# S5 state space layer: the products "powers times B" one f tile ahead, and the states turned into matmul operands by a ScalarE copy and a trip through DRAM

## The chip, the core and the metric

The kernel runs on one NeuronCore of a Trainium2 chip. The metric is the device time of one execution in microseconds (us). In the names used here TensorE is PE (the matrix engine; PEld is its weight load), VectorE is DVE, ScalarE is ACT, GpSimd is POOL and SyncE is SP. A matmul's result lands in PSUM, everything else that an engine reads or writes lies in SBUF, both with 128 partitions; weights and intermediate arrays lie in DRAM and move by DMA. Each engine works through its own list of instructions in order and waits for the others by semaphores. PE, DVE and ACT compute; SP only issues DMAs, and ACT and POOL can issue them too.

## The reference

Two layers, each a token mixer in a wide projection with a gate, then a residual and a LayerNorm: first chunked gated linear attention (GLA), then a complex diagonal state space layer (S5). The change lies in the second. Cut to what matters:

```python
# u_in: (1, 256, 2048); 256 groups of 16 channels, 64 complex states each
u, z = jnp.split(u_in @ w_in, 2, axis=-1)              # 2048 -> 4096 and 4096
dt = jnp.exp(log_dt)[:, None]
lam = exp(a_re * dt) * (cos(a_im * dt) + i sin(a_im * dt))   # written out in real parts
bb = (lam - 1) / (a_re + i a_im) * b                   # per group 64 x 16, complex
bu = einsum('blgi,gpi->blgp', u, bb)
x_l = lam * x_{l-1} + bu_l                             # associative_scan over 256 frames
y = einsum('blgp,gip->blgi', x_r, c_re) - einsum('blgp,gip->blgi', x_i, c_im) + d_skip * u
y = jax.nn.gelu(y)
y = y * jax.nn.sigmoid(y @ w_glu + b_glu)
return (y * jax.nn.silu(z)) @ w_out
```

The first half of `w_in`'s columns gives the input u, the second half the gate z.

## The kernel before, in words

**Weights.** All large weight matrices are float32 and are streamed once, in tiles of 128 partitions x 1024 (512 KB each, loaded by SP, L134). `split` makes two parts of each tile: `hi`, a copy rounded to the format fp32r (an ACT cast, L145), and `lo`, the rest (a DVE subtraction, L146). The activations are kept in the same two parts. A product is then three fast matmuls, hi x hi, lo x hi and hi x lo (`st_step`, L180 to L182, 24 matmuls for one weight tile). There are four buffers for the loaded tiles and three each for `hi` and `lo`. For every step of a projection ACT must cast, DVE must subtract, and only then PE can end the step.

**The S5 layer's recurrence** is cut into 32 chunks of 8 frames. The 4096 channels make 32 f tiles of 128 channels (8 groups of 16), and 16 pairs p of such tiles. Within a chunk everything is a matrix product, and only the state at the chunk's end goes from chunk to chunk. This needs, for each f tile:
- "powers times B" (`b_pow`): B times eight powers of lambda. One ACT copy and three DVE products (L1096 to L1098, by `powmul`'s and `b_pow`'s lines) make the buffer `wb` from the record `rb`.
- `b_tr`: eight PE transposes of it (L1107) into PSUM `pswb`, and two ACT copies.
- `s_mm` for a pair: matmuls for the chunks' own state and for the kernel of the first eight frames, PSUM `pss`; a DVE transpose (L1139) puts the states into `sx`, the large state array.
- `k_out`: the kernel of eight frames goes out to DRAM (`dk`).
- `scan`: 30 steps for each half h of the f tiles, three small DVE instructions each (L1187 to L1189), in place in `sx`.
- `cside`: the records of C and lambda are loaded (`cl`, three DMAs), the block Toeplitz operand `mt` is read back from `dk` (L1233, 512 KB, two buffers), and `powmul` makes C times powers (`wc0`, `wc1`).
- `xstage` (L1238 to L1247): the states of the chunks' starts are made an operand: a DVE transpose from `sx` to `xT` (L1241), two PE transposes to PSUM `psxs` (L1244), an ACT copy to `xS` (L1246).
- `ystage` (L1249 to L1263): 24 matmuls in PSUM `psy` (8 with `mt`, L1256, 16 with `wc` and `xS`, L1259), a DVE transpose to `yt` (L1262), and gelu on ACT back into `U` (L1263).

**What runs when.** This work runs in the gaps of two projections of 8 groups g by 8 steps kp. The input projection `su` (L1198 on) takes a queue `bq` of the B work: `bstep` runs as many entries at each step as `b_pace` allows, which is set to -4 at the start of g = 1 (so the queue starts some steps later, when u's first tiles are there) and gains 1 a step. From g = 4 on, `pump` also runs scan steps of half 0. The gate projection `sz` (L1274 on) ends the queue in g = 0 and then pumps a second queue `bg`, filled in the order of f: up to three scan steps of half 1, `cside(f)`, `xstage(f - 1)`, `ystage(f - 2)`; `Y_RATE` = 2.311 entries a step. The gate's silu (L1284, `zs`) stands at the end of each g.

The order in which this text runs gives a priority; a scheduler then sets each engine's list from the priorities, its own costs of instructions and the buffers' turnover, so the lists may differ from the text. Buffers are tiles of pools: a tile with `bufs=n` takes the n places in turn and waits until the place is free. `s8` is a pool of 12 large places that `wu`, `wb`, `U`, `zs` and others share.

Of the kernel before, what the change touches and what calls it, by code (L numbers as in the profile page):

```python
# [15 lines left out]
P = 128  # L16
# [17 lines left out]
def trunk(ctx, tc, x, c, ln_g, ln_b, ada_w, ada_b, gla_w_in, gla_gate_w2, gla_gate_b, gla_norm_g,  # L34
# [394 lines left out]
    vt = cp.tile([P, 104], F32, name="vt")  # L429
    gnT, gbT, bgluT, lngT, lnbT = vt[:, 0:32], vt[:, 32:40], vt[:, 40:72], vt[:, 72:88], vt[:, 88:104]  # L430

    def vectors():
# [8 lines left out]
        S.copy(vt, ps[:, :104])  # L441

# [5 lines left out]
    abT = cp.tile([P, 64], F32, name="abT")  # L448
# [22 lines left out]
    dT = cp.tile([16, 256], F32, name="dT")  # L471

    def prep_small():
# [5 lines left out]
        S.copy(dT, ps[:16, 0:256])  # L479
# [121 lines left out]
    def prep_pow(t):  # L601
# [14 lines left out]
        wdma(rec[:, 16 * t:16 * t + 16, 128:256], lc.rearrange("p f r g n -> p f (r g n)"))  # L616

    def to_rows(src, i_of, t, o, nm):
        got = {}

        def step(ib):
# [7 lines left out]
            if ib == 3:  # L629
                av = a.rearrange("p (f g) i -> p f (g i)", f=16)  # L630
                wdma(rec[:, 16 * t:16 * t + 16, o:o + 128], av)

        return [lambda ib=ib: step(ib) for ib in range(4)]

    def prep_b(t):
# [22 lines left out]
        return [load], [comp] + to_rows(lambda: got["b"], lambda s, i: s[:, :, i], t, 256, f"b{t}")  # L658

    def prep_c(t):  # L660
# [15 lines left out]
        return [load], [comp] + to_rows(lambda: got["c"], lambda s, i: s[:, i].rearrange("g r p -> g (r p)"), t, 0, f"c{t}")  # L676
# [15 lines left out]
    Y_RATE = 2.311  # L692
# [360 lines left out]
    def bload(f2):  # L1053

        a = tp.tile([P, 2, 384], F32, tag="rb", name=f"rb{f2}", bufs=2)
        dma(a[:, :, 0:256], rec[:, 2 * f2:2 * f2 + 2, 128:384])
        for h in range(2):
            dma(a[64 * h:64 * h + 64, :, 256:384], rec[64 - 64 * h:128 - 64 * h, 2 * f2:2 * f2 + 2, 256:384])
        rb[f2] = a
# [3 lines left out]
    def kload(f2):  # L1063

        a = rc[f2] = tp.tile([P, 2, 144], F32, tag="rc", name=f"rc{f2}", bufs=2)
        dma(a, rec[:, 2 * f2:2 * f2 + 2, 0:144])

    wb = {}
# [10 lines left out]
    wu, kts, Upair = {}, {}, {}  # L1079

    def b_pow(f):
        p = f // 2
        if f % 2 == 0:
# [3 lines left out]

            wu[p] = s8t(f"wb{p}", [2, 8, 16, 8])
        a = rb[p][:, f % 2]
        w = wu[p][:, f % 2]  # L1090
# [9 lines left out]
    def b_tr(f):  # L1100
        p = f // 2
        if f % 2 == 0:
            wb[p] = s8t(f"wbt{p}", [2, 8, 128])
        for h in range(2):
            ps = psx(f"pswb{f}{h}")
            for g in range(4):
                PE.transpose(ps[:, g * P:(g + 1) * P], wu[p][:, f % 2, 4 * h + g].rearrange("p i s -> p (i s)"), ident)  # L1107
            S.copy(wb[p][:, f % 2, 4 * h:4 * h + 4, :], ps.rearrange("p (g r) -> p g r", g=4))
# [10 lines left out]
    def s_mm(p):  # L1119
        pss = [psx(f"pss{2 * p + i}") for i in range(2)]  # L1120
        for i in range(2):
# [4 lines left out]
            for b in range(2):  # L1126
                for q in range(4):
                    PE.matmul(pss[i][32 * q:32 * q + 32, b * P:(b + 1) * P], lhsT=U[:, 2 * q + b],
                              rhs=wb[p][:, i, 2 * q + b, :], start=True, stop=True)
# [326 lines left out]
```

## Time and profile before

| | |
|---|---|
| time, median of 3 runs | 1836.67 us (1836.52 to 1839.31) |
| profiled execution | 1838.83 us, span 1837.1 us |
| granted TensorE clock, mean | 0.991 |
| ACT, POOL busy | 895.4 us (49%), 88.0 us (5%) |
| DMA | 457.86 MB, 249 GB/s over the span; 437.01 MB read, 18.61 MB written |
| of the chain that ended last | PE 78%, DVE 11%, DMA 4%, issue 3%, ACT 2% |

Busy time is the sum of an engine's instructions; an engine that is not busy either waits for a semaphore or for its own issue. A window is a stretch of the span in microseconds from its start; its row gives the length, then each engine's busy time with the count of its instructions, the granted clock, the mean busy share of the 16 DMA engines and the rate. A row of waits reads: waiting engine, tile and line, releaser with its tile and line, then microseconds in total, times, longest. A row of groups reads: line, engine, operation, output and input with their sizes, count, busy time in us, mean ns of one, and idle time before it with what ended it. Timeline rows begin with start and duration. The stages that the change touches lie, by the first and last matmul of each, at 762 to 1019 us (`su`) and 1021 to 1289 us (`sz`).

### The profile page before, as it was taken

To read this page: it belongs to the slowest core of one execution; us is meant where nothing else is said; L and a number is where in the kernel's file an instruction comes from. 1 tells how busy PE (TensorE), PEld (TensorE's weight loads), DVE (VectorE), ACT (ScalarE), POOL (GpSimd) and SP (SyncE) were. 2 spreads that over 40 slices of the span, in tenths; PEclk is the share of its full clock that TensorE was granted. 3 is DMA by queue.
4 is the path that set the end of the run, shared out by engine and by line. 5 is a ranking of instruction groups with operands and counts; after the bars stand their busy time and mean duration, and the time that the engine had idled before them with its cause. 6 is when DMAs were issued, how large, how long until landed. Compare 5 with 4: busy or idle time off the path is not lost.

```text
span 1837.1 us, 33664 instructions
## 1 busy us (share of the span) xinstructions
PE 1781.8 (97%) x13491; PEld 1574.5 (86%) x13491; DVE 1410.3 (77%) x1880; ACT 895.4 (49%) x1266; POOL 88.0 (5%) x94
## 2 busy tenths in 40 slices
PE   7999999999999999999999999999999999999997
PEld 5776897899999888899998999988888888888886
DVE  4887757879999988687699689888577775557556
ACT  4433557556556333654554535545445444444332
POOL 0000000000000000002233300000000000000000
PEclk9999999999999999999999999999999999999998
DMA  9997975879889998486665577999688886668653
GB/s 343 387 342 247 294 247 162 284 258 325 290 289 321 335 356 289 160 264 204 194 202 168 170 213 217 234 246 233 218 278 269 275 271 208 187 192 324 194 185 92
DMA packets 246101, 457.86 MB, mean 249 GB/s; under 512 B 19828, under 2 KB 49198, under 8 KB 244662
## 3 DMA queue, kind: packets, MB, share of 16 engines
q1 hardware_dynamic: 239320, 436.02, 74.1%
q0 software_dynamic: 5856, 18.63, 3.1%
q8 instruction: 106, 1.74, 0.4%
q10 hardware_dynamic: 768, 1.05, 0.2%
q14 instruction: 51, 0.42, 0.1%
HBM read 437.01 MB, written 18.61 MB: 248 GB/s over the span
## 4 chain that ended last, share of the span: by engine, by line
PE 78%; DVE 11%; DMA 4%; issue 3%; ACT 2%; POOL 0%; SPq 0%; DVEq 0%; ACTq 0%; POOLq 0%
PE gl L192 13%; PE gl L193 7%; PE op L168 6%; PE op L169 6%; PE op L167 6%; PE z L182 3%; PE z L181 3%; PE z L180 3%; PE v L168 3%; PE v L169 2%; PE v L167 2%; PE su L180 2%; PE su L181 2%; PE su L182 2%; PE sz L180 2%
## 5 line engine op out<-in xcount | busy, mean ns | idle before, releaser
L146 DVE TENSOR_TENSOR logl<-wgl,higl 128x1024 fp32r<-128x1024 f32 x128 | 156.7, 1224 | 116.0 <-ACT higl L145 111.2
L145 ACT CAST higl<-wgl 128x1024 fp32r<-128x1024 f32 x128 | 134.4, 1051 | 172.4 <-PE gl L192 167.5
L192 PE MATMUL gl<-yp,higl 128*128 128x512 f32 x512 | 179.4, 395 | 0.1
L192 PE MATMUL gl<-yb,higl 128*128 128x512 f32 x512 | 179.1, 395 | 0.0
L145 ACT CAST hio<-wo 128x1024 fp32r<-128x1024 f32 x95 | 100.2, 1055 | 152.8 <-PE op L169 131.9
L146 DVE TENSOR_TENSOR loo<-wo,hio 128x1024 fp32r<-128x1024 f32 x95 | 116.5, 1228 | 66.8 <-ACT hio L145 64.8
L317 DVE SCALAR_TENSOR_TENSOR acc<-wa,cs,acc 128x512 f32<-128x512 f32 x217 | 162.7, 750 | 2.9 <-DMA wa<-in_ada_w 0.2
L180 PE MATMUL sz<-u1h,hisz 128*128 128x256 f32 x512 | 150.4, 294 | 2.3 <-ACT zs L1284 2.3
L180 PE MATMUL su<-u1h,hisu 128*128 128x256 f32 x512 | 151.3, 297 | 0.0
L180 PE MATMUL z<-u0h,hiz 128*128 128x256 f32 x512 | 148.7, 290 | 0.0
L182 PE MATMUL sz<-u1h,losz 128*128 128x256 f32 x512 | 144.5, 283 | 2.1 <-DVE losz L146 2.1
L182 PE MATMUL su<-u1h,losu 128*128 128x256 f32 x512 | 145.8, 285 | 0.0
L181 PE MATMUL su<-u1l,hisu 128*128 128x256 f32 x512 | 145.6, 284 | 0.0
L182 PE MATMUL z<-u0h,loz 128*128 128x256 f32 x512 | 144.9, 283 | 0.6 <-DVE loz L146 0.6
L181 PE MATMUL z<-u0l,hiz 128*128 128x256 f32 x512 | 144.7, 283 | 0.0
L181 PE MATMUL sz<-u1l,hisz 128*128 128x256 f32 x512 | 144.7, 283 | 0.0
L193 PE MATMUL gl<-yb,logl 128*128 128x256 f32 x512 | 143.0, 279 | 0.0
L193 PE MATMUL gl<-yp,logl 128*128 128x256 f32 x512 | 142.3, 279 | 0.0
L145 ACT CAST hisz<-wsz 128x1024 fp32r<-128x1024 f32 x64 | 67.0, 1049 | 113.6 <-PE sz L181 57.4
L192 PEld LDWEIGHTS gl<-yp,higl 128*128 128x128 f32 x512 | 95.9, 188 | 22.9 <-issue 0.6
L192 PEld LDWEIGHTS gl<-yb,higl 128*128 128x128 f32 x512 | 96.0, 188 | 22.6
L145 ACT CAST hiz<-wz 128x1024 fp32r<-128x1024 f32 x64 | 67.2, 1051 | 88.2 <-PE z L181 80.8
(322 smaller groups left out, 5000.8 us busy)
## 6 DMA issues: line engine op xcount, KB each, us to landing
wgl<-in_s_w_glu SPq DMA_DIRECT2D x128, 512.0 KB, 4.8
wa<-in_ada_w SPq DMA_DIRECT2D x116, 512.0 KB, 5.2
wv<-in_gla_w_in SPq DMA_DIRECT2D x64, 512.0 KB, 6.5
wz<-in_gla_w_in SPq DMA_DIRECT2D x64, 512.0 KB, 5.4
wsu<-in_s_w_in SPq DMA_DIRECT2D x64, 512.0 KB, 4.5
wsz<-in_s_w_in SPq DMA_DIRECT2D x64, 512.0 KB, 5.7
wo<-in_s_w_out SPq DMA_DIRECT2D x64, 512.0 KB, 4.7
a<-in_ada_w SPq DMA_DIRECT2D x31, 1024.0 KB, 10.7
```

The costliest lines, as they stand in the source:

```text
L145: S.copy(hi, w)
L146: last_lo[0] = V.tensor_tensor(lo, w, hi.bitcast(F32), op=ALU.subtract).ins
L167: PE.matmul(banks[tt], lhsT=uh, rhs=hi[:, kk, :], start=(k == first), stop=False)
L168: PE.matmul(banks[tt], lhsT=uh, rhs=lo[:, kk, :], start=False, stop=False)
L169: last_mm[0] = PE.matmul(banks[tt], lhsT=ul, rhs=hi[:, kk, :], start=False, stop=(k == last)).ins
L180: PE.matmul(o, lhsT=wh, rhs=u.hi(k), start=(k == first), stop=False)
L181: PE.matmul(o, lhsT=wh, rhs=u.lo(k), start=False, stop=False)
L182: last_mm[0] = PE.matmul(o, lhsT=wl, rhs=u.hi(k), start=False, stop=(k == last)).ins
L192: PE.matmul(banks[f], lhsT=hi[:, kk, fs], rhs=u.both(k), start=(k == 0), stop=False)
L193: PE.matmul(banks[f][:, :T], lhsT=lo[:, kk, fs], rhs=u.hi(k), start=False, stop=(k == last))
L317: V.scalar_tensor_tensor(acc[0], w[:, kk, :], cs[:, k:k + 1], acc[0], op0=ALU.mult, op1=ALU.add)
```

## The change

- **B one f tile ahead.** The queue `bq` gets a first entry `b_pow(0)`, and the entry of tile f now runs `b_pow(f + 1)` and `b_tr(f)`. `b_pace` starts at -3 for the additional entry. The targets `wu` and `wb` become two fixed buffers each, taken in turn by p, where each pair took a new place of the pool before.
- **States by copy and DRAM.** `xstage` goes. `xwrite(f)` copies the states from `sx` to `xT` on ACT (three buffers) and writes them to a DRAM array `dx` from ACT's own DMA queue (128 KB); `xread(f)` reads them back in the operand's layout to `xS` (three buffers) by POOL's queue, in pieces of 64 floats. In `bg`, `xwrite(0)` and `xwrite(1)` stand at f = 0, `xwrite(f + 1)` at f, and `xread(f)` behind them: four entries for each f where there were three, apart from scans. `Y_RATE` becomes 2.9.
- **C records.** The record `rec` has 512 floats instead of 384: C is written a second time with its halves of the partitions exchanged, by two more DMAs per writing. `cload` is then one DMA of 128 rows instead of three. The partitions of C, lambda and the states come in the order (frame of the chunk, part) instead of (part, frame), by the pattern of the load.
- **Buffers.** `yt` has one buffer instead of two; `vt` and `abT` lie in a pool that is closed early, and `bgluT` is copied out of `vt`; `dT` goes out to DRAM (`dd`) and is loaded where it is used.

The diff, cut to its core:

```diff
+    bgluT = cp.tile([P, 32], F32, name="bgluT")
...
-    rec = dp.tile([P, 32, 384], F32, name="rec")
+    rec = dp.tile([P, 32, 512], F32, name="rec")
...
+    dx = dp.tile([32, P, 256], F32, name="dx")
...
+                if o == 128:
+                    for h in range(2):
+                        wdma(rec[64 * h:64 * h + 64, 16 * t:16 * t + 16, 0:128], av[64 - 64 * h:128 - 64 * h])
...
-    Y_RATE = 2.311
+    Y_RATE = 2.9
...
+    wu = [s8t(f"wu{i}", [2, 8, 16, 8]) for i in range(2)]
+    wb = [s8t(f"wbt{i}", [2, 8, 128]) for i in range(2)]
...
-    bq = []
+    bq = [lambda: b_pow(0)]
...
-                bq.append(lambda f=f: (kload(f // 2) if f % 2 else None, b_pow(f), b_tr(f)))
+                bq.append(lambda f=f: (kload(f // 2) if f % 2 else None, b_pow(f + 1) if f < 31 else None, b_tr(f)))
...
-                b_pace[0] = -4.0
+                b_pace[0] = -3.0
...
-        dma(a[:, 0:256], rec[:, f, 0:256])
-        for h in range(2):
-            dma(a[64 * h:64 * h + 64, 256:384], rec[64 - 64 * h:128 - 64 * h, f, 0:128])
+        dma(a, rec[:, f, 0:384].rearrange("(r l) x -> l r x", r=4))
...
-    def xstage(f):
-        xt_ = tp.tile([P, 2, 4, 32], F32, tag="xt", name=f"xT{f}", bufs=1)
+    def xwrite(f):
+        xt_ = tp.tile([P, 4, 2, 32], F32, tag="xt", name=f"xT{f}", bufs=3)
         n = 2 * (f % 16)
-        V.transpose(xt_, sx[:, f // 16, 0:32, :, n:n + 2].rearrange("p c r b -> p b r c"))
-        px = psx(f"psxs{f}")
-        for b in range(2):
-            PE.transpose(px[:, b * P:(b + 1) * P], xt_[:, b].rearrange("p r l -> p (r l)"), ident)
-        xs = tp.tile([P, 2, 128], F32, tag="xs", name=f"xS{f}", bufs=2)
-        S.copy(xs, px[:, :T].rearrange("p (b r) -> p b r", b=2))
-        xss[f] = xs
+        S.copy(xt_, sx[:, f // 16, 0:32, :, n:n + 2].rearrange("p c r b -> p r b c"))
+        S.dma_start(dx[f], xt_.rearrange("p r b c -> p (r b c)"))
+
+    def xread(f):
+        xs = xss[f] = tp.tile([P, 4, 2, 32], F32, tag="xs", name=f"xS{f}", bufs=3)
+        wdma(xs.rearrange("p q b c -> p q (b c)"), dx[f].rearrange("(q l) (r x) -> (l r) q x", q=4, r=4))
...
-        yt = tp.tile([P, 8, 32], F32, tag="yt", name=f"yt{f}", bufs=2)
+        yt = tp.tile([P, 8, 32], F32, tag="yt", name=f"yt{f}", bufs=1)
...
-                if 1 <= f < 33:
-                    bg.append(lambda f=f: xstage(f - 1))
+                for i in range(0 if f == 0 else f + 1, min(f + 2, 32)):
+                    bg.append(lambda i=i: xwrite(i))
+                if f < 32:
+                    bg.append(lambda f=f: xread(f))
```

How it moves the instructions. First DVE's list in the input projection, where g = 4 passes into g = 5 (`losu46` is the subtraction for g = 4's step 6; `pt16` and `pt17` are products for the tiles 16 and 17; `sca10` is the first scan step). Before:

```order
L1098 TENSOR_TENSOR wb7_9347<-wb7_9347,pt15_9399 128x128x7
L1097 TENSOR_TENSOR pt16_9574<-rb8_9343 128x896
L146 TENSOR_TENSOR losu46_9418<-wsu46_9415,hisu46_9417 128x1024
L146 TENSOR_TENSOR losu47_9461<-wsu47_9458,hisu47_9460 128x1024
L1139 STREAM_TRANSPOSE sx_7542<-pss12_9274 128x2x4x32
L1139 STREAM_TRANSPOSE sx_7542<-pss13_9275 128x2x4x32
L146 TENSOR_TENSOR losu50_9541<-wsu50_9538,hisu50_9540 128x1024
```

In the changed kernel, the same place:

```order
L1143 STREAM_TRANSPOSE sx_7551<-pss12_9284 128x2x4x32
L1143 STREAM_TRANSPOSE sx_7551<-pss13_9285 128x2x4x32
L1102 TENSOR_TENSOR wu0_7558<-rb8_9190 128x128x7 x2
L1104 TENSOR_TENSOR wu0_7558<-wu0_7558,pt16_9407 128x128x7
L1103 TENSOR_TENSOR pt17_9577<-rb8_9190 128x896
L146 TENSOR_TENSOR losu50_9549<-wsu50_9546,hisu50_9548 128x1024
L1104 TENSOR_TENSOR wu0_7558<-wu0_7558,pt17_9577 128x128x7
L1103 TENSOR_TENSOR pt18_9638<-rb9_9402 128x896
```

Before, the products of tile 16 that follow `pt16` (L1096, L1098) stand sixteen rows further down, behind the subtractions of g = 5's steps 0 to 3 and the first scan steps; now both products of tile 16 and those of tile 17 stand ahead of g = 5's second step.

Second, ACT's list in the gate projection at g = 4, steps 4 to 6 (`hisz44` is the cast of step 4, `U` the gelu of an f tile). Before:

```order
L145 CAST hisz44_12923<-wsz44_12921 128x1024
L1263 ACT_TABLE_LOAD
L1263 ACTIVATE U0_7545<-yt7_12721 128x8x32
L1246 COPY xS9_12769<-psxs9_12766 128x256
L145 CAST hisz45_12991<-wsz45_12989 128x1024
L1263 ACTIVATE U1_7546<-yt8_12796 128x8x32
L1246 COPY xS10_12844<-psxs10_12841 128x256
L145 CAST hisz46_13066<-wsz46_13064 128x1024
```

In the changed kernel between the casts of the steps 5 and 6:

```order
L145 CAST hisz45_12961<-wsz45_12959 128x1024
L1245 COPY xT24_13773<-sx_7551 128x256
L1245 COPY xT25_13844<-sx_7551 128x256
L1246 DMA dx_205<-xT24_13773 128x256
L1246 DMA dx_205<-xT25_13844 128x256
L1245 COPY xT26_13915<-sx_7551 128x256
L1246 DMA dx_205<-xT26_13915 128x256
L1245 COPY xT27_14016<-sx_7551 128x256
L1246 DMA dx_205<-xT27_14016 128x256
L145 CAST hisz46_13002<-wsz46_13000 128x1024
```

Where one copy `xS` followed one gelu, the copies now come in clusters: the sixteen of half 1 stand between the casts of g = 4's step 2 and step 7, those of half 0 in g = 1 and g = 2, and each copy is followed by a DMA that ACT issues.

Third, PE's list in the same projection, at f tile 18. Before:

```order
L1244 MATMUL psxs19_13615<-ident_89,xT19_13613 128x128 x2
L1256 MATMUL psy18_13620<-mt18_13427,U2_7547 32x128 x4
L1259 MATMUL psy18_13620<-wc018_13429,xS18_13513 32x128 x4
L1259 MATMUL psy18_13620<-wc118_13430,xS18_13513 32x128 x4
L1256 MATMUL psy18_13620<-mt18_13427,U2_7547 32x128 x4
```

In the changed kernel:

```order
L1259 MATMUL psy18_13527<-mt18_13314,U2_7556 32x128 x4
L1262 MATMUL psy18_13527<-wc018_13316,xS18_13353 32x128 x4
L1262 MATMUL psy18_13527<-wc118_13317,xS18_13353 32x128 x4
L1259 MATMUL psy18_13527<-mt18_13314,U2_7556 32x128 x4
```

The pair of transposes that stood ahead of each tile's `psy` group is gone; the group itself is the same 24 matmuls.

More of the change, by code (lines that the diff above doesn't have):

```diff
@@ L427, in vqk_steps @@
         return steps
-    vt = cp.tile([P, 104], F32, name="vt")
-    gnT, gbT, bgluT, lngT, lnbT = vt[:, 0:32], vt[:, 32:40], vt[:, 40:72], vt[:, 72:88], vt[:, 88:104]
+    vt = rp.tile([P, 104], F32, tag="vt", name="vt")
+    bgluT = cp.tile([P, 32], F32, name="bgluT")
+    gnT, gbT, bglu_, lngT, lnbT = vt[:, 0:32], vt[:, 32:40], vt[:, 40:72], vt[:, 72:88], vt[:, 88:104]
     def vectors():
@@ L441, in vectors @@
         S.copy(vt, ps[:, :104])
+        S.copy(bgluT, bglu_)
     ada0 = ada_now(0, 0, 0, 2)
@@ L447, in trunk @@
         dma(vr2[32 * l:32 * l + 32, :], ada_b[l, 0:4096].rearrange("(k p) -> k p", p=P))
-    abT = cp.tile([P, 64], F32, name="abT")
+    abT = rp.tile([P, 64], F32, tag="abT", name="abT")
     ps = psx("psv2")
@@ L478, in prep_small @@
             PE.transpose(ps[:16, h * P:(h + 1) * P], dr[:, h, :], ident)
-        S.copy(dT, ps[:16, 0:256])
+        dt_ = rp.tile([16, 256], F32, tag="row", name="dt_", bufs=2)
+        S.copy(dt_, ps[:16, 0:256])
+        wdma(dd, dt_)
         zt = rp.tile([P, 448], F32, tag="row", name="zt", bufs=2)
```

38 lines of the change are left out of this document (18 added, 20 removed).

## The prediction

> **What bounds the kernel now.** I read the busy line of the page first, then a table of windows over the two stages that the change touches, then what TensorE (PE) waits for in them, then single stretches of its timeline, then the DMA issues.
>
> ```profile
> PE 1781.8 (97%) x13491; PEld 1574.5 (86%) x13491; DVE 1410.3 (77%) x1880; ACT 895.4 (49%) x1266; POOL 88.0 (5%) x94
> ```
>
> PE is busy for 97% of the span, so a change gains only where it takes matrix work away or ends a PE wait. The windows, in order: the first and second part of the input projection `su` with the products "powers times B"; then the gate projection `sz`, its first part, in which VectorE (DVE) still scans the second half, and its second part, after the scan.
>
> ```profile
> core 0: us, PE busy (x) PEld busy (x) DVE busy (x) ACT busy (x) POOL busy (x), PEclk, DMA share, GB/s
> 789.90:919.00 129.10, 129.06 (x1444) 123.86 (x1443) 94.03 (x95) 69.01 (x128) 28.09 (x33) 1.00 0.71 216
> 919.00:1021.20 102.20, 97.95 (x1076) 93.28 (x1074) 99.87 (x166) 50.75 (x96) 33.98 (x27) 0.98 0.63 189
> 1062.60:1153.40 90.80, 86.87 (x1031) 83.10 (x1030) 87.56 (x155) 40.82 (x58) 0.00 (x0) 1.00 0.79 223
> 1153.40:1286.20 132.80, 127.63 (x1845) 119.13 (x1845) 115.32 (x132) 69.69 (x113) 0.00 (x0) 0.99 0.96 238
> ```
>
> Each stage has another second limit. From 919 to 1021 us DVE is full (99.87 of 102.20 us), and again from 1062 to 1153 us (87.56 of 90.80 us). From 1153 us on DVE has room, and the DMA engines are 96% busy. PE itself loses 0.04, 4.25, 3.93 and 5.17 us in the four rows (length less busy time). What it waits for, in the input projection and then in the gate projection (us in total, times, longest):
>
> ```profile
> PE pswb L1107 <- DVE wb L1098: 4.7, 3, 3.1
> ```
>
> ```profile
> PE psy L1256 <- DMA mt<-dk: 5.1, 3, 2.1
> PE sz L180 <- ACT zs L1284: 2.3, 3, 1.7
> PE sz L182 <- DVE losz L146: 2.1, 1, 2.1
> ```
>
> So 14.2 us of waits stand in the stages concerned; the rest of any gain must come from matrix work.
>
> **The change, part by part.** *The PE transposes of the states go.* The timeline of PE around one pair:
>
> ```profile
> 1143.26 0.28 PE L182 MATMUL sz<-u1h,losz 128*128 128x256 f32 x1
> 1143.38 0.38 PE L1244 MATMUL psxs<-ident,xT 128*128 128x128 f32 x2
> 1143.52 0.36 PE L180 MATMUL sz<-u1h,hisz 128*128 128x256 f32 x1
> 1143.72 0.28 PE L181 MATMUL sz<-u1l,hisz 128*128 128x256 f32 x1
> 1143.84 0.28 PE L182 MATMUL sz<-u1h,losz 128*128 128x256 f32 x1
> ```
>
> Starts, not durations, tell the price: projection matmuls follow each other at 0.12 us (1143.72 to 1143.84). From L182 to the L181 after the pair it is 0.46 us, without the pair it would be 0.24. A pair costs 0.22 us, 32 pairs 7.0 us, of which 10 pairs (2.2 us) lie before 1153 us and 22 (4.8 us) after. I take **-7.0 us**; this is PE's own work and nothing hides it, except where PE then waits for a transfer (below).
>
> *Powers times B one tile ahead.* One tile is three DVE products and one ScalarE (ACT) copy:
>
> ```profile
> L1096 DVE TENSOR_TENSOR wb<-rb 128x896 f32<-128x896 f32 x32 | 34.7, 1094 | 1.4 <-DMA rb<-rec 1.4
> L1098 DVE TENSOR_TENSOR wb<-wb,pt 128x896 f32<-128x896 f32 x32 | 34.7, 1084 | 0.2
> L1097 DVE TENSOR_TENSOR pt<-rb 128x896 f32<-128x896 f32 x32 | 34.7, 1084 | 0.2
> ```
>
> No work is removed. 3.26 us of DVE work moves ahead by one tile, out of the full window into the one before, where DVE has 35 us to spare (129.10 less 94.03). That is a little more than the longest wait (3.1 us). Upper bound: the 4.7 us, and the clock that dips to 0.98 in the row of that wait (2% of 102.2 us, 2.0 us): 6.7 us. Lower bound: nothing, if the full DVE is then late with `losu` instead of `wb`. I take **-5.0 us**, since the shift is as long as the wait. The two transposes that land in `sx` hold DVE to PE's pace as before, so the shared buffers `wu` and `wb` add no wait of their own. SP's `rb` load keeps its place behind the same products.
>
> *DVE loses the state transposes, ACT gets a copy in their place.*
>
> ```profile
> L1241 DVE STREAM_TRANSPOSE xT<-sx 128x256 f32<-128x256 f32 x32 | 20.3, 636 | 0.3
> L1246 ACT COPY xS<-psxs 128x256 f32<-128x256 f32 x32 | 11.5, 359 | 0.9 <-PE psxs L1244 0.9
> L628 ACT COPY rowsc<-psrc 128x512 f32<-128x512 f32 x8 | 8.6, 1071 | 0.0
> L1263 ACT ACTIVATE U<-yt 128x256 f32<-128x256 f32 x32 | 13.3, 415 | 11.8 <-DVE yt L1262 11.7
> L1284 ACT ACT_TABLE_LOAD x10 | 12.8, 1283 | 0.2
> L145 ACT CAST hisz<-wsz 128x1024 fp32r<-128x1024 f32 x53 | 55.5, 1049 | 94.9 <-PE sz L181 44.8 <-issue 36.8 <-DMA wsz<-in_s_w_in 11.8
> ```
>
> DVE's full window before 1153 us loses 10 x 0.636 = 6.4 us. The waits on `losz` (2.1) and on `zs`, an ACT instruction that stands behind a gelu waiting for DVE, (2.3) come from it: -4.4 us at best, 0 if ACT's new work makes `zs` late again. I take **-3.5 us**.
>
> ACT gives up 32 x 0.359 us and takes 32 copies from `sx` with a stride of 512 B. No row shows that read. Bounds: 0.36 us (`xS`) and half of L628's 1.071 us, a strided copy of twice the size, 0.54 us; I take 0.5. Each is followed by a DMA issue on ACT, which on SP takes 0.34 to 0.54 us:
>
> ```profile
> 1173.22 0.34 SPq L1217 DMA_DIRECT2D cl<-rec  x1
> 1173.62 1.40 SPq L1219 DMA_DIRECT2D cl<-rec  x2
> 1175.33 0.54 SPq L1233 DMA_DIRECT2D mt<-dk  x1
> ```
>
> So a state costs ACT about 0.95 us. By the order these come in two bursts, 16 among seven casts `hisz` and 16 among six. Second burst: 16 x 0.95 + 6 x 1.05 + 4 gelus x 0.42 + a table load of 1.28 = 24.5 us of ACT. PE needs for those six steps 6 x 24 x 0.12 = 17.3 us and four `psy` groups of 1.6 us (below), 23.8 us. Even; but the copies have three buffers, and a fourth waits until the first's write has landed. With a landing of L one copy takes (L + 0.95)/3. Queued behind such a wait on ACT are the casts, then DVE's `losz`, then PE. For L there are these rows, 128 KB and 64 KB, over the whole run and in the second part of `sz`:
>
> ```profile
> out<-big ACTq DMA_DIRECT2D x16, 64.0 KB, 2.1
> cl<-rec SPq DMA_DIRECT2D x32, 128.0 KB, 3.6
> ...
> wsz<-in_s_w_in SPq DMA_DIRECT2D x24, 512.0 KB, 8.2
> mt<-dk SPq DMA_DIRECT2D x22, 512.0 KB, 9.0
> cl<-rec SPq DMA_DIRECT2D x20, 128.0 KB, 7.6
> ```
>
> L = 3.6 gives 24 us for 16 copies, no loss. L = 7.6 gives 46 us; three `hi` buffers let ACT fall back by about two steps (8 us), and 14 us are lost. ACT's writes do not queue behind SP's own, so I stand near 3.6: **+2 us** (0 to 14).
>
> *The transfers.* One tile's C rows come in one DMA of 128 rows of 1.5 KB instead of three with 256 shorter rows: same bytes, and two SP issues fewer ahead of `mt`. Added are 128 KB out (ACT's queue) and 128 KB back (POOL's queue, in 256 B pieces) per tile. Up to 1153 us the share of 0.79 hides them. After that:
>
> ```profile
> DMA packets 17689, 31.59 MB, mean 238 GB/s; under 512 B 1844, under 2 KB 7220, under 8 KB 17670
> ```
>
> ```profile
> DMA packets 2941, 5.46 MB, mean 273 GB/s; under 512 B 291, under 2 KB 1059, under 8 KB 2939
> q1 hardware_dynamic: 2939, 5.43, 101.9%
> ```
>
> The first is 1153 to 1286 us, the second 1190 to 1210 us, the fastest 20 us that I found in it (its queue q1 full, 101.9%). 22 tiles in 132.8 us are 6.0 us and 1.44 MB each. The change adds 0.131 MB per tile read and 16 x 0.131 MB written, in all 1.66 MB. `mt` has two buffers, so a load issued after one `psy` must land before the second next; where three follow each other step by step PE already waits:
>
> ```profile
> 1207.61 0.43 PE L1256 MATMUL psy<-mt,U 128*32 128x128 f32 x8
> 1208.51 0.62 PE L1259 MATMUL psy<-wc,xS 128*32 128x128 f32 x16
> 1209.06 0.38 PE L180 MATMUL sz<-u1h,hisz 128*128 128x256 f32 x1
> ...
> 1214.51 0.66 PE L1256 MATMUL psy<-mt,U 128*32 128x128 f32 x8 [2.10 <-DMA mt<-dk]
> ```
>
> (The first three give a `psy` group its length: 1207.61 to 1209.06, with the changeover 1.6 us.) Two such steps without transposes are 9.0 us (2 x (2.88 + 1.6)), as long as `mt` takes to land. Best case: the waits of 5.1 us end, since `cl` is lighter and the pace of 2.9 steps over four items per tile instead of three spreads the groups (24 in the last 31 steps; before 26 in 30). Worst: the path gives no more than 238/0.96 = 248 GB/s, 6.7 us per tile, 15 us more than now. At 273 GB/s it is 6.1 us, 2 us more than now, and the late transposes' 4.8 us are not seen. I take the point nearer to 273 GB/s, for the short rows of `cl` go: **+4 us** on the sum, which leaves this window 0.8 us shorter than now.
>
> The rest hides: C rows written a second time, in half-sized DMAs of 0.5 MB, four in all, go out in a stretch with PE 98% busy and a DMA share of 0.78 (row below); uncovered, 2 MB at 248 GB/s would be 8 us. The one copy of `bgluT` and the load of `dT` stand beside work that waits anyway. **+0.5 us**.
>
> ```profile
> 200.00:300.00 100.00, 98.19 (x661) 88.24 (x660) 61.49 (x79) 62.27 (x71) 6.34 (x6) 1.00 0.78 248
> ```
>
> **Sum**: -7.0 - 5.0 - 3.5 + 2 + 4 + 0.5 = -9.0 us. The profiled execution took 1838.83 us (span 1837.1), 2.2 us over the median; 1829.8 for such an execution, and 1836.67 - 9 = **1828 us** for the median.
>
> **The rivals.** *The DMA engines become the bound (slower).* Place: `sz` after the scan, PE waiting for `mt` at `psy`. At 248 GB/s the window grows by 15 us, and of the rest stay -5.0 - 3.5 - 2.2 + 2 + 0.5: +7, **1843 us**. It decides against the change where a tile takes over 6.4 us, under 259 GB/s. For it: share 0.96 and landings twice as long as elsewhere. Against: 273 GB/s over 20 us. A form of it is that the 256 B pieces take the engines twice their bytes' time: 22 x 0.131 MB more at 273 GB/s, 10.6 us, with the 2 us of that rate +12.6, 1841 us. The Trainium skill (DMA: Bandwidth & Descriptors, Specifications) states such a loss: full rate from 512 B, below it a read-modify-write. No row here has data pieces under 512 B, so the trace neither agrees nor differs.
>
> *ACT takes the place of DVE (no change).* Landings of 7 us instead of 3.6: 16 x 7.95/3 = 42.4 us, less 31.8, 10.6 lost instead of 2: **1836 us**. For it: the late landings of `cl`. Against: they sit behind SP's own loads.
>
> *The change doesn't do what it says (no change).* DVE stays full, `losu` and `losz` are late instead of `wb`, and both waits stay: 8.5 us of the sum fall away, **1836 us**. For it: no DVE work leaves the input projection.
>
> *All waits go*: 7.0 + 6.7 + 4.4 + 5.1 = 23 us, 1814 us.
>
> **How the numbers follow.** Forecast 0.52 (its own range 1822 to 1833), all waits go 0.10, ACT 0.08, not as said 0.08, DMA 0.22 (0.07 of it the 256 B form). A measurement here can tell about 0.2%, 3.7 us, from no change: faster 0.62, same 0.16, slower 0.22. The range leaves out the outer half of the best and of the worst case: 1817 to 1844 us.
>
> **What would show it.** In the profile after: `pswb` without a wait on DVE, and no new wait on `losu` beside it; DVE clearly under full from 1062 to 1153 us; no PE wait on `zs` or `losz`; ACT's idle time in the bursts put down to DMA writes of `dx` (rival two if it exceeds 10 us); rate over 270 GB/s in the late window, with `mt` landing at 9 us or less. The forecast is wrong if PE waits for `mt` grow beyond 15 us, or `xS` is ever waited for: it has two tiles' time to arrive.

## The result, and the profile after

The changed kernel takes 1860.67 us (median of four runs), against 1837.99 us for the kernel before in the same comparison: a ratio of 1.0121 with a 95% interval of 1.0104 to 1.0137, so 22 us slower (19 to 25). Forecast was 1828 us, and its range ended at 1844. One of the four runs was disturbed (2905.43 us at a granted clock of 0.557) and is not in the ratio; the median of the other three is 1859.23.

First the places in the span. These are rows of single tiles: line, engine, operation, count, shortest, median and longest duration in ns, then the first and last start in us. Before, with `z` the gate projection of the GLA layer, `su` and `sz` the two projections of the S5 layer:

```profile
L180 PE MATMUL z<-u0h,hiz x512: 280/283/681, 366.8 to 578.1; 128*128 128x256 f32 x171
L180 PE MATMUL su<-u1h,hisu x512: 277/283/562, 762.5 to 1018.8; 128*128 128x256 f32 x171
L182 PE MATMUL su<-u1h,losu x512: 278/283/415, 763.7 to 1019.1; 128*128 128x256 f32 x171
L180 PE MATMUL sz<-u1h,hisz x512: 277/283/583, 1021.2 to 1288.6; 128*128 128x256 f32 x171
L182 PE MATMUL sz<-u1h,losz x512: 277/283/386, 1021.5 to 1288.8; 128*128 128x256 f32 x171
```

The same tiles in the changed kernel:

```profile
L180 PE MATMUL z<-u0h,hiz x512: 277/283/682, 373.3 to 584.7; 128*128 128x256 f32 x171
L180 PE MATMUL su<-u1h,hisu x512: 277/283/562, 769.3 to 1020.5; 128*128 128x256 f32 x171
L182 PE MATMUL su<-u1h,losu x512: 278/283/562, 770.6 to 1020.8; 128*128 128x256 f32 x171
L180 PE MATMUL sz<-u1h,hisz x512: 277/283/583, 1022.9 to 1312.0; 128*128 128x256 f32 x171
L182 PE MATMUL sz<-u1h,losz x512: 278/283/583, 1023.2 to 1312.3; 128*128 128x256 f32 x171
```

From the first L180 to the last L182, `su` went from 256.6 to 251.5 us, as forecast (-5.1). But `z` starts 6.5 us later, in a part of the kernel for which the prediction had half a microsecond, and `sz` grew from 267.6 to 289.4 us (+21.8). Everything after it is unchanged. -5.1 + 6.5 + 21.8 is the 23.2 us between the two spans.

What PE waits for in `sz` of the changed kernel (us in total, times, longest):

```profile
PE psy L1259 <- DMA mt<-dk: 19.2, 9, 4.3
PE sz L180 <- ACT zs L1287: 6.7, 1, 6.7
PE sz L182 <- DVE losz L146: 4.2, 5, 2.0
PE sz L180 <- ACT hisz L145: 1.5, 1, 1.5
```

Before, these were 5.1 us for `mt`, 2.3 for `zs` and 2.1 for `losz`. Two of the rivals show at the same time: the DMA engines (`mt`), and ACT (`zs`, `hisz`, and `losz` behind them). What ACT itself waits for, and the group of the new copies:

```profile
ACT xT L1245 <- DMA dx<-xT: 22.9, 15, 4.7
```

```profile
L1245 ACT COPY xT<-sx 128x256 f32<-128x256 f32 x32 | 20.6, 657 | 25.5 <-DMA dx<-xT 22.9 <-ACT xT L1245 2.2 <-DMA dk<-ks 0.2
```

A copy waits for the landing of the third write before it, 22.9 us in total. The end of the first burst, on ACT's timeline (start, duration), shows who stands behind it:

```profile
1087.17 1.04 ACT L145 CAST hisz<-wsz 128x1024 fp32r<-128x1024 f32 x1
1087.30 0.33 ACTq L1246 DMA_DIRECT2D dx<-xT  x1
1091.13 0.65 ACT L1245 COPY xT<-sx 128x256 f32<-128x256 f32 x1 [2.92 <-DMA dx<-xT]
1091.81 0.33 ACTq L1246 DMA_DIRECT2D dx<-xT  x1
1092.18 0.94 ACT L1287 ACTIVATE zs<-sz 128x256 f32<-128x256 f32 x3 [0.40 <-ACT xT L1245]
```

`zs`, which frees the PSUM of the last group, is ready to run, but the last copy of the burst stands ahead of it and waits 2.92 us for a landing. PE stands still for 6.69 us, until 1092.62. And at the other limit, the DMA engines in the part after the scan (1155 to 1290 us: packets, then issues with size and median us to landing):

```profile
DMA packets 16575, 33.88 MB, mean 251 GB/s; under 512 B 1656, under 2 KB 6257, under 8 KB 16558
```

```profile
mt<-dk SPq DMA_DIRECT2D x21, 512.0 KB, 11.2
xS<-dx POOLq DMA_DIRECT2D x21, 128.0 KB, 8.4
dx<-xT ACTq DMA_DIRECT2D x14, 128.0 KB, 4.2
```

`mt` takes 11.2 us to land where it took 9.0. The windows of `sz` (length, busy time of PE, PEld, DVE, ACT and POOL, then granted clock, DMA share, GB/s) add a third loss:

```profile
1064.00:1155.00 91.00, 81.65 (x946) 77.87 (x949) 79.21 (x138) 44.50 (x62) 8.29 (x11) 0.96 0.85 247
1155.00:1200.00 45.00, 39.42 (x548) 36.65 (x537) 28.62 (x30) 25.63 (x37) 4.64 (x7) 0.96 0.91 260
1200.00:1280.00 80.00, 69.53 (x986) 64.90 (x985) 60.13 (x64) 33.48 (x48) 9.57 (x13) 1.00 1.04 242
1280.00:1312.30 32.30, 25.20 (x359) 23.19 (x358) 22.50 (x29) 14.61 (x22) 1.50 (x2) 0.84 0.79 200
```

DVE is no longer full, PE is not either, and the clock, 0.99 or 1.00 in these stages before, is 0.96 and at the end 0.84.

### The profile page after: what moved, and what is told of

Same layout as the page of the kernel before. It is cut to its first block, busy times and chain, and to the rows that moved or that the text cites. A ratio compares the mean times of both kernels' runs of the same rounds, so it can differ in the third digit from the quotient of the medians.

```text
span 1860.3 us, 33501 instructions
## 1 busy us (share of the span) xinstructions
PE 1783.2 (96%) x13427; PEld 1575.1 (85%) x13427; DVE 1396.5 (75%) x1848; ACT 905.1 (49%) x1263; POOL 116.1 (6%) x131
## 5 line engine op out<-in xcount | busy, mean ns | idle before, releaser
L180 PE MATMUL sz<-u1h,hisz 128*128 128x256 f32 x512 | 151.0, 295 | 8.2 <-ACT zs L1287 6.7
L180 PE MATMUL su<-u1h,hisu 128*128 128x256 f32 x512 | 151.6, 297 | 0.0
L182 PE MATMUL sz<-u1h,losz 128*128 128x256 f32 x512 | 146.4, 287 | 4.2 <-DVE losz L146 4.2
L180 PE MATMUL z<-u0h,hiz 128*128 128x256 f32 x512 | 148.7, 290 | 0.0
L182 PE MATMUL su<-u1h,losu 128*128 128x256 f32 x512 | 145.8, 285 | 0.5 <-DVE losu L146 0.5
L182 PE MATMUL z<-u0h,loz 128*128 128x256 f32 x512 | 144.9, 283 | 0.6 <-DVE loz L146 0.6
L180 PEld LDWEIGHTS sz<-u1h,hisz 128*128 128x128 f32 x512 | 99.5, 194 | 15.2 <-ACT zs L1287 7.3
```

Source lines behind the costliest of these rows:

```text
L180: PE.matmul(o, lhsT=wh, rhs=u.hi(k), start=(k == first), stop=False)
L182: last_mm[0] = PE.matmul(o, lhsT=wl, rhs=u.hi(k), start=False, stop=(k == last)).ins
```

## The experiments

All runs in one table. The ratio is to the kernel before on the same chip; `z` is the start of the GLA layer's gate projection, `su` and `sz` the lengths of the two S5 projections in the one profiled execution, all in us.

| run | time | ratio (95%) | z | su | sz |
|---|---|---|---|---|---|
| before | 1837.99 | 1 | 366.8 | 256.6 | 267.6 |
| changed | 1860.67 | 1.0121 (1.0104 to 1.0137) | 373.3 | 251.5 | 289.4 |
| e1 B ahead alone | 1826.10 | 0.9940 (0.9923 to 0.9956) | 365.9 | 252.3 | 262.7 |
| e2 changed, old states | 1837.09 | 1.0006 (0.9995 to 1.0017) | 374.5 | 250.5 | 264.3 |
| e3 changed, three reads | 1849.05 | 1.0070 (1.0054 to 1.0085) | 373.5 | 250.2 | 275.6 |
| e4 changed, 32 copy buffers | 1843.71 | 1.0050 (1.0033 to 1.0068) | 373.7 | 250.3 | 271.6 |
| e5 both of these | 1834.24 | 0.9987 (0.9972 to 1.0003) | 372.5 | 253.0 | 255.4 |
| e6 reads in whole rows | 1858.67 | 1.0118 (1.0097 to 1.0139) | 374.2 | 250.6 | 283.9 |
| e7 second C copy late | 1853.70 | 1.0086 (1.0067 to 1.0105) | 369.6 | 250.3 | 286.2 |
| e8 B ahead, pace 2.9 | 1828.65 | 0.9956 (0.9941 to 0.9971) | 366.7 | 249.9 | 263.6 |
| e9 before once more | 1837.60 | one run | 365.2 | 256.1 | 266.6 |
| e10 as e5, three writes | 1835.40 | 1.0003 (0.9985 to 1.0022) | 373.0 | 250.2 | 264.1 |
| e11 changed, both mended | 1837.46 | 1.0023 (1.0002 to 1.0045) | 368.4 | 250.5 | 270.0 |
| e12 B ahead, no transposes | 1822.51 | 0.9928 (0.9902 to 0.9953) | 365.6 | 250.8 | 259.3 |
| e13 as e1 | 1829.63 | 0.9961 (0.9946 to 0.9977) | 366.2 | 252.4 | 264.2 |

### Which part of the change costs what: e1, e2

**e1**: the kernel before, with B one tile ahead and nothing else.

```diff
+    wu = [s8t(f"wu{i}", [2, 8, 16, 8]) for i in range(2)]
+    wb = [s8t(f"wbt{i}", [2, 8, 128]) for i in range(2)]
...
-    bq = []
+    bq = [lambda: b_pow(0)]
...
-                bq.append(lambda f=f: (kload(f // 2) if f % 2 else None, b_pow(f), b_tr(f)))
+                bq.append(lambda f=f: (kload(f // 2) if f % 2 else None, b_pow(f + 1) if f < 31 else None, b_tr(f)))
...
-                b_pace[0] = -4.0
+                b_pace[0] = -3.0
```

> The kernel before, with only the products "powers times B" one f tile ahead (fixed wu and wb, pace -3). The input projection was 256.6 us before (762.5 to 1019.1) and 251.5 in the change. If that step alone did this, the projection takes about 251.5 us here too, everything else is as before, and the time is 1838 - 5 = 1833 us. If the gain needed the other edits, the projection stays at 256 us and the time at 1838.

Measured: 0.9940 of before, 11 us faster (8 to 14). `su` is 4.3 us shorter, as expected; `sz`, where the step changes no work, is 4.9 us shorter too. This kernel is faster than both the one before and the changed one.

**e2**: the changed kernel with the old `xstage` put back, as one entry for each f; B ahead, the doubled C record and the pace of 2.9 stay.

```diff
-    def xwrite(f):
...
+    def xstage(f):
+        xt_ = tp.tile([P, 2, 4, 32], F32, tag="xt", name=f"xT{f}", bufs=1)
...
-        dma(a, rec[:, f, 0:384].rearrange("(r l) x -> l r x", r=4))
+        dma(a, rec[:, f, 0:384])
```

> The changed kernel, with the states made an operand as before (DVE transpose, two PE transposes, ACT copy); B ahead, the C record written twice, one load of it per tile and the pace of 2.9 stay. Theory A, the copy and the trip through DRAM cost the gate projection its 21.8 us: it takes about 268 us again, and what is left over is the 6.6 us that the stages before the input projection lost, so 1861 - 22 = 1839 us. Theory B, the pace of 2.9 or the single C load does it: the projection stays near 285 us and the time near 1857.

Measured: 1837.09 us, 264.3 us for `sz`. Theory A holds: the copy and the trip through DRAM cost `sz` its time (a ratio of 1.0121 falls to 1.0006, 21 us), not the pace and not the single C load. And e2 loses against e1 almost only before the input projection: `z` starts at 374.5 instead of 365.9 us.

### Bytes or ACT: e3, e4, e5, e10

**e3** leaves the reads back out but for three:

```diff
     def xread(f):
+        if f > 2:
+            xss[f] = xss[f % 3]
+            return
```

> The changed kernel without the reads of the states from DRAM but for the first three f tiles, whose operands all later tiles use (so 29 of the 32 tiles compute with other states); copies and writes stay. Theory 1, the DMA engines pace the part after the scan: 2.9 MB less there at 238 GB/s are 12 us, the waits for mt fall from 19 to 7 us or less, and the time is 1849. Theory 2, ACT blocked behind the landing of its writes does it: nothing changes there, 1859 to 1861.

**e4** gives each copy a buffer of its own, in `wu` and `wb`:

```diff
-        xt_ = tp.tile([P, 4, 2, 32], F32, tag="xt", name=f"xT{f}", bufs=3)
+        xt_ = (wu + wb)[f // 8].rearrange("p a b i s -> p (a b i s)" if f < 16 else "p a b r -> p (a b r)")[:, (f % 8) * 256:(f % 8 + 1) * 256].rearrange("p (r b c) -> p r b c", r=4, b=2)
```

> The changed kernel with a buffer of its own for each of the 32 copied states (in wu and wb, which are no longer used then), so that no copy on ACT waits for an earlier write to land; same bytes. Theory 2 (ACT blocked): ACT's 22.9 us of waits on dx go, and with them PE's waits on zs (6.7), most on losz and on hisz, so -8 to -14 us, 1847 to 1853. Theory 1 (DMA paces): the waits move to mt, and the time stays within 4 us of 1860.

Measured: both theories are right, each for its part. Without the reads the time falls by 9 us (1.0121 to 1.0070) and `sz` by 13.8; with the buffers by 13 us (to 1.0050) and `sz` by 17.8. PE's waits in e3:

```profile
PE sz L180 <- ACT zs L1290: 5.6, 2, 5.2
PE sz L182 <- DVE losz L146: 5.0, 6, 2.0
PE psy L1262 <- DMA mt<-dk: 4.4, 4, 1.3
PE psy L1262 <- DVE wc L1083: 3.7, 1, 3.7
```

and in e4, with ACT's own wait for landings, which was 22.9 us:

```profile
PE psy L1259 <- DMA mt<-dk: 13.1, 6, 4.2
PE sz L182 <- DVE losz L146: 3.6, 1, 3.6
ACT wbt L1245 <- DMA dx<-wbt: 4.4, 2, 2.8
```

Each takes away its own wait and leaves most of the other: without reads PE waits 4.4 us for `mt` instead of 19.2 and still 5.6 for `zs`, with the buffers not at all for `zs` instead of 6.7 and still 13.1 for `mt`. Without reads a wait of 3.7 us for `wc` appears. The wait for `mt` falls from 19.2 to 13.1 us with the buffers at the same bytes, so ACT's lag had a part in it. **e5** does both (the edits of e3 and e4).

> The changed kernel with a buffer for each copied state (as in the run with thirty-two copies) and with three reads only (as in the run with three reads; 29 of the 32 tiles compute with other states). The gate projection took 289.4 us in the changed kernel, 275.6 with three reads, 271.6 with the buffers, 264.3 with the old states. If bytes and ACT's block are two separate costs, both away leave the old states' time less the 7 us of PE transposes, 257 us, and the time is 1861 - 32 = 1829. If they are one cost, each removing what the other would (ACT is blocked because the engines are full), it stays near 268 us, time 1840.

Measured: 0.9987, 25 us less than the changed kernel by the ratios; 9 and 13 apart add to 22. They add, as two separate costs do; if they were one cost, both away would give little more than 13. The time itself, 1834 us, lies between the two that were expected, 1829 and 1840. The profiled execution took 1828.78 us, 5 us under the median, so its 255.4 us for `sz` may be up to 5 us short of the usual. **e10** also leaves out the writes, but for three:

```diff
-        S.dma_start(dx[f], xt_.rearrange("p r b c -> p (r b c)"))
+        if f < 3:
+            S.dma_start(dx[f], xt_.rearrange("p r b c -> p (r b c)"))
```

> As the run with both (a buffer for each copy, three reads only), and now only the first three of the 32 states are written to DRAM, too; the copies on ACT stay (29 of 32 tiles compute with other states). If each byte in the gate projection costs what the reads cost (3.8 MB gave 14 to 16 us), the other 3.8 MB give as much again, 1834 - 14 = 1820. If the engines have room once the reads are gone, nothing changes: 255 us for the gate projection, 1832 to 1835.

Measured: 1.0003, no gain over e5 by the times. Once the reads are gone, the bytes of the writes cost nothing that the times show. That `sz` is 8.7 us longer than in e5 is for the larger part the spread of single executions: e5's profiled execution took 1828.78 us, e10's 1836.08. The rest is open.

### The pieces of 256 B: e6

**e6** reads each state back in rows of 1 KB, in the order in which it was written.

```diff
-        wdma(xs.rearrange("p q b c -> p q (b c)"), dx[f].rearrange("(q l) (r x) -> (l r) q x", q=4, r=4))
+        wdma(xs.rearrange("p q b c -> p (q b c)"), dx[f])
```

> The changed kernel with each read of the states from DRAM in 128 rows of 1 KB instead of 512 pieces of 256 B; the operand is then not in the order that the product needs (the state's share of y is another), bytes and count of reads are the same. If pieces of 256 B take the DMA engines twice their bytes' time, 22 x 0.131 MB at 238 GB/s, 12 us, are saved: gate projection 277 us, time 1848. If pieces cost by their bytes, nothing changes: 289 us, 1859 to 1861.

Measured: 1.0118 against 1.0121, no difference in time; 12 us would be 0.0065. `sz` is 5.5 us shorter in the profile, less than half of the 12 us, and the two profiled executions differ by 5.2 us in all (1862.11 and 1856.91) where the ratios do not. POOL's queue in the part after the scan (packets, MB, share of the engines), in the changed kernel and then in e6:

```profile
q0 software_dynamic: 976, 2.69, 8.6%
```

```profile
q0 software_dynamic: 1008, 2.75, 7.8%
```

The count of packets under 512 B tells nothing of these pieces: it is 1656 in the changed kernel and 1707 in e6. For the same bytes the small pieces take a share of 8.6 instead of 7.8%, a tenth more, not twice as much. The rule of the Trainium skill (DMA: Bandwidth & Descriptors, Specifications) that pieces under 512 B lose full rate to a read-modify-write is not borne out for this read from DRAM at anything like the factor of two that the rival was priced with.

### What happens ahead of the S5 layer: e7, e11

In the changed kernel POOL issues the exchanged C copy right behind the first writing, in two DMAs of 0.5 MB; the second pair comes at 351.18 us (start and duration of the issue):

```profile
351.18 1.66 POOL L639 DMA_DIRECT2D rec<-rowsc  x2
```

The first gate weights `wz` are loaded then. ACT's wait for them before the copies `sts` of the GLA states, in the kernel before, in the changed one, and in e7:

```profile
360.40 1.99 ACT L145 CAST hiz<-wz 128x1024 fp32r<-128x1024 f32 x2 [3.93 <-DMA wz<-in_gla_w_in]
```

```profile
368.37 1.99 ACT L145 CAST hiz<-wz 128x1024 fp32r<-128x1024 f32 x2 [8.23 <-DMA wz<-in_gla_w_in]
```

```profile
364.60 1.99 ACT L145 CAST hiz<-wz 128x1024 fp32r<-128x1024 f32 x2 [5.72 <-DMA wz<-in_gla_w_in]
```

Behind these casts stand ACT's copies `sts`, and PE's next product waits for them. **e7** makes the copy later, from DRAM to DRAM.

```diff
-                if o == 128:
-                    for h in range(2):
-                        wdma(rec[64 * h:64 * h + 64, 16 * t:16 * t + 16, 0:128], av[64 - 64 * h:128 - 64 * h])
...
     dma(dT, dd)
+    for h in range(2):
+        wdma(rec[64 * h:64 * h + 64, :, 0:128], rec[64 - 64 * h:128 - 64 * h, :, 128:256])
```

> The changed kernel with the second, exchanged copy of the C records made by two DMAs from DRAM to DRAM just before the input projection, instead of right behind each first writing. If these writes delay the loads of the first gate weights of the GLA layer (ACT waited 8.2 us for wz instead of 3.9), that projection starts at 368 or 369 us instead of 373.3, and the time falls by 4 to 6 us, to 1855. If the other edits of the preparation do it (copies of dT and of the biases), it stays at 373 us, 1860.

Measured: `z` starts at 369.6 us instead of 373.3, and the time is 6 us less by the ratios (1.0086; the two intervals still touch, at 1.0104 to 1.0105). By the profile the copy is the cause of 3.7 of the 6.5 us. The other 2.8 us belong to edits of the preparation that were not tried one by one.

**e11** is the changed kernel, complete, with the edits of e4 and e7 together.

> The changed kernel, complete, with the two faults that can be mended taken away together: a buffer for each copied state and the exchanged C copy made late by DRAM-to-DRAM DMAs. The two runs apart gave -16 and -6 us; if they add, 1861 - 23 = 1838, no better than before, since the reads' 14 to 16 us stay. If the late copy only moved the cost, 1843.

Measured: 1.0023 (1.0002 to 1.0045). The two add (18 us by the ratios, 13 and 6 apart), and what then remains is no better than before: the reads and the rest of the preparation use up about what B ahead and the transposes give.

### The gains by themselves: e8, e9, e12, e13

**e8**: e1 with the pace of 2.9.

```diff
-    Y_RATE = 2.311
+    Y_RATE = 2.9
```

> The kernel before with B one tile ahead, and the pace of 2.9 entries a step where 2.311 was (the entries are the old three per tile, so the outputs come earlier). If a faster pace fills the stretch in which the DMA engines still have room, the waits for mt and so the gate projection fall by 1 to 2 us, 1824 to 1825; if DVE, full during the scan, pays for it, PE waits on losz and zs grow by 2 to 5 us, 1828 to 1831.

Measured: 1828.65 us, `sz` 263.6. The ratio of 0.9956 lies between those of the two runs without it (e1 0.9940, e13 0.9961), so the pace by itself, with three entries for each tile, has no effect that these runs show. **e9** is the kernel before, unchanged, for a second profile.

> The kernel before once more, for a second profile of it: how far its stages move between executions. If stage times repeat to a microsecond, the gate projection takes 267 to 268 us and the GLA layer's gate projection starts at 366 to 367 us, and the 262.7 us of the gate projection with B ahead alone are an effect of that step; if it is at 263 to 265 us here, that part was the spread of single profiles.

Measured: stage lengths repeat within 1 us (`su` 256.1, `sz` 266.6), the starts within 2. **e12** is e1 without the 64 PE transposes; **e13** is e1 again beside it.

```diff
-        px = psx(f"psxs{f}")
-        for b in range(2):
-            PE.transpose(px[:, b * P:(b + 1) * P], xt_[:, b].rearrange("p r l -> p (r l)"), ident)
...
-        S.copy(xs, px[:, :T].rearrange("p (b r) -> p b r", b=2))
+        S.copy(xs, xt_.rearrange("p b r l -> p b (r l)"))
```

> The kernel before with B one tile ahead, and without the 64 PE transposes of the states (ACT copies the operand straight from DVE's block transpose, so the state's share of y is another); everything else as before, no trip through DRAM. It measures the disputed gain by itself, beside the same kernel with the transposes. If each pair costs PE 0.22 us that nothing hides, the gate projection and the time are 7 us shorter than with them. If PE waits for mt in their place in the part where the DMA engines are full (22 of the 32 pairs), only 2 to 3 us are seen.

> The kernel before with B one tile ahead, once more on this chip, as the measure for the run without transposes, and for the gain of this step: first 1826.1 us, 0.994 of before, with 252.3 us for the input and 262.7 us for the gate projection. If the gate projection's 4 to 5 us belong to the step, it is at 262 to 264 us again and the ratio at 0.993 to 0.996; if they were the spread of one profile, it is at 267 us.

Measured: 1822.51 against 1829.63 us, 7.1 us by the medians and 6 by the ratios. The rows of `sz` in e13 and then in e12:

```profile
L180 PE MATMUL sz<-u1h,hisz x512: 277/283/387, 1016.4 to 1280.3; 128*128 128x256 f32 x171
```

```profile
L180 PE MATMUL sz<-u1h,hisz x512: 277/283/387, 1014.2 to 1273.3; 128*128 128x256 f32 x171
```

264 us became 259: 5 of the 7 us are seen in the stage itself. The transposes are real work on the path, worth about what the sum said; the two intervals overlap a little (0.9902 to 0.9953 and 0.9946 to 0.9977). And e13 repeats e1: `su` 252.4, `sz` 264.2, a ratio of 0.9961. So B ahead gives 4 us in `su` and about 3 in `sz`, together 7 to 11.

## Why the prediction was wrong, point by point

*PE transposes, -7.0 us.* Right in mechanism, and in size as far as e12 tells: 7.1 us by the medians, 5 in the stage. In the changed kernel the gain is there, but buried.

*B one tile ahead, -5.0 us.* Right in place and size (`su` -5.1; PE's wait of 4.7 us on `wb` is gone, and the one on `losu` beside it is 0.5 us), and too small in all: e1 and e13 give 11 and 7 us, since `sz` is shorter as well. Why that is was not found.

*DVE relief, -3.5 us.* Wrong. The waits that it was to end grew: `zs`, `hisz` and `losz` took 12.4 us instead of 4.4. That DVE was busy for only 79.21 of 91.00 us from 1064 on is no relief: it stood still behind ACT (its waits for `hisz` in `sz` rose from 21.4 to 40.1 us). With both costs away (e5) it is nearly as full in the same window as before the change, when it was busy for 87.76 us:

```profile
1064.00:1155.00 91.00, 87.69 (x1036) 84.37 (x1039) 86.12 (x147) 43.17 (x58) 1.44 (x2) 0.98 0.84 241
```

There PE no longer waits for `zs`, but 3.3 us for `losz`, so about 1 us of the 3.5 is seen. In the changed kernel, what was put down as the lower bound, 0 "if ACT's new work makes `zs` late again", is what came about.

*ACT's bursts, +2 us (0 to 14).* Here the first large piece is lost: e4 gets 13 us back by the times. The landing of a write was put at 3.6 us and took 4.2 in the median (3.9 in the first burst); a copy was put at 0.5 us and took 0.66. That is not much: with 3.9 us and 1.0 us for a copy and its issue, the rule gives 16 x 4.9/3 = 26 us for a burst. The step that failed is that the loss was worked out for the second burst alone, which has four `psy` groups on PE to hide it. The first burst has none: seven steps of `sz` are 7 x 2.88 = 20 us of PE. The sixteen copies, with the casts between them, took 31 us, from 1061.08 to 1091.78; their group from 1060 to 1093 us has 12.5 us of waits for landings:

```profile
L1245 ACT COPY xT<-sx 128x256 f32<-128x256 f32 x16 | 10.4, 655 | 13.4 <-DMA dx<-xT 12.5 <-ACT xT L1245 0.6 <-DMA dk<-ks 0.2
```

At their end `zs`, which had not been listed as queued behind the copies of this burst, waited with them. So the 8 us by which the `hi` buffers were to let ACT fall back did not help: at the end of a group PE needs `zs` first. The copies took 11 us longer than PE's work, and PE waited 9.4 us for `zs` and `losz` between 1064 and 1155 us. Three buffers were the cause and not ACT's work, since with 32 buffers the same copies cost PE no wait for `zs`.

*The transfers, +4 us.* The second piece: the reads alone cost 9 us by the times (e3; 12 from e4 to e5), 14 in the profile. This term of the sum was mis-sized. By the forecast's own working a rate of 273 GB/s makes the window 2 us longer and hides the 4.8 us of the late transposes, +6.8 on the sum, so +4 was below even that. The rival of the DMA engines named the place (`psy`, waiting for `mt`), the price (15 us) and the point from which it decides (under 259 GB/s); the window shows 251 GB/s and `mt` at 11.2 us, and the waits of 19.2 us are over the 15 that were to refute the forecast. The choice of the 273 GB/s of one good stretch of 20 us, over the 238 of the whole stage, is the step that failed. Its form with pieces of 256 B fell (e6). But a mean rate is not the whole account. With a buffer for each copy (e4) the same transfers went at 270 GB/s:

```profile
1155.00:1280.00 125.00, 113.91 (x1624) 106.17 (x1616) 96.13 (x102) 60.70 (x88) 14.95 (x20) 0.96 1.03 270
```

There `mt` landed in 9.1 us in the median, so both signs that the forecast asked for are nearly there, and PE still waited 13.1 us for `mt`. What makes single `mt` loads late at such a rate, these runs do not show.

*The rest, +0.5 us.* The third: 6.5 us at the start of `z`, 3.7 of it by the second C copy (e7). The cover was read from a window of 200 to 300 us with a DMA share of 0.78; the second of the two writings came at 351 us, ahead of a burst of weight loads. A mean share over 100 us did not tell what these 4 us held.

*The rivals as alternatives.* The forecast gave ACT 0.08 and the DMA engines 0.22, one or the other. Both came, because both hang on the same added transfers, and the range ended where one of them alone would have ended. Neither rival with its own sum (1836 and 1843) nor the range held 1861. Added up, the DMA rival (+7), what the ACT rival puts on top of the sum (+8.6) and the 6 us of e7 are about 22 us. That this is the measured loss is partly luck: the -3.5 us of the DVE term is still in it, and the lost clock is not.

*What no term held.* After some of its waits PE runs at half its clock (last section). An estimate from windows of 0.5 us over `sz`, PE's busy time times the share of the clock that was missing, gives 7.4 us lost in the changed kernel, 1.6 before and 1.7 in e5. So about 6 of the 21.8 us of `sz` are lost clock, and the waits alone do not show them. With the 7 us of transposes gone, PE's busy time over the kernel still rose from 1781.8 to 1783.2 us. From e2 to the changed kernel the ratios differ by 21 us, and taking away both costs gives 25 back; the 3.5 us below e2 that remain are less than the 7 that e12 shows. That remainder is within what these intervals tell, and was not followed further.

## What to carry to other kernels

A ring of n buffers in front of a DMA holds the engine that fills it to at most n items in one landing time and its own work, and whatever else stands in that engine's list pays: work the sum out for every burst, the one with the least other work on the bottleneck first, and list all that is queued behind. Where a transfer is added to a stage whose DMA engines are full, price it by the rate of the whole stage, not of its best stretch, and look at the landing of the load that is waited for, since the mean rate alone does not tell. Where two rivals hang on the same added transfers, add their prices for the upper end of the range. A change that bundles a gain with a trade should be timed in its parts: here B ahead alone, a few lines, was 0.4 to 0.6% faster than before, while the whole was 1.2% slower.

## What the runs showed of the hardware

The granted clock halves after long waits, and once after short ones. The stretch behind the 6.69 us, in the changed kernel:

```profile
1092.60:1096.50 3.90, 3.88 (x18) 3.89 (x18) 2.73 (x7) 3.43 (x6) 0.00 (x0) 0.50 0.46 141
```

The clock is 0.50 for 3.9 us, so by half of that time, some 2 us, this wait cost more than it lasted. At the end of `sz` two waits stand close together:

```profile
1296.83 0.65 PE L1259 MATMUL psy<-mt,U 128*32 128x128 f32 x8 [4.29 <-DMA mt<-dk]
1301.62 0.66 PE L1259 MATMUL psy<-mt,U 128*32 128x128 f32 x8 [2.01 <-DMA mt<-dk]
```

```profile
1296.80:1302.00 5.20, 3.16 (x56) 2.77 (x60) 1.98 (x2) 0.00 (x0) 0.00 (x0) 0.50 0.90 235
1302.00:1306.00 4.00, 4.00 (x57) 3.62 (x49) 2.77 (x6) 1.46 (x3) 0.00 (x0) 0.55 0.63 166
```

These stretches make the 0.84 of the last window in the section on the result. The Trainium skill (TensorE: Matmul & The Clock Gate, Part 1: The HAM clock gate) states that the clock falls to a half after idle windows of about 3.4 us and takes about as long to come back; the trace agrees for the waits of 6.69 and 4.29 us. Single waits of 3.02 us (until 1211.26) and 2.59 us (until 1173.57) left the clock at 1.00. But from 1186.5 to 1189.5 us it is 0.50 behind waits of only 1.48 and 0.76 us, 1.3 us apart, so the longest wait alone does not tell when it falls.

A full DMA share is no fixed rate. With a share of 1.04 the changed kernel moved 242 GB/s (1200 to 1280 us). With the same kinds of transfer e4 moved 270 with a share of 1.03 (1155 to 1280 us, above), and e5, with only the first three reads back, moved more than the changed kernel with a smaller share:

```profile
1155.00:1278.90 123.90, 120.32 (x1795) 112.89 (x1788) 105.08 (x115) 65.78 (x97) 0.00 (x0) 1.00 0.96 262
```

And an ACT copy of 128 x 256 from `sx`, with a stride of 512 B, takes 0.657 us; the copy of the same size from PSUM took 0.359 before, and one from SBUF without that stride takes 0.406 in e12.
